# A Hymba layer on one core: the far blocks of attention exponentials are transposed by VectorE and a trip through memory

## The chip, the cores and the metric

The kernel runs on one core of a Trainium2 chip. The core has a TensorE (PE: matmuls; its weight loads are listed apart as PEld), a VectorE (DVE), a ScalarE (ACT), a GpSimd engine (POOL) and a SyncE (SP), which in this kernel issues most DMAs. Each engine works through its own instructions in order; between engines semaphores decide. The metric is the device time of one launch in microseconds (us); lower is better. Three runs of the kernel before gave 1260.56, 1261.29 and 1263.95 us, median 1261.29.

## The reference, cut to what matters

One layer over 1024 positions of width 1024. The change touches only the attention; the DeltaNet branch `B`, the convolutions and the norms are left out here.

```python
u = rms_norm(h, mix_norm_gain)
proj = u @ w_in                     # queries, keys, values of 8 heads of 64; q, k, v, gate of 4 DeltaNet heads
...
# A: each chunk of 64 positions sees itself and the 8 chunks before it
scores = einsum('bcqhd,bckhd->bchqk', qc, kb) * 64 ** -0.5 + bias[rel_idx]
scores = where(valid, scores, finfo.min)
p = softmax(scores, axis=-1)
o = einsum('bchqk,bckhd->bcqhd', p, vb)
o_att = rms_norm(o)
...
h = h + concat([o_att, o_dn], axis=-1) @ w_out
h = h + square(relu(rms_norm(h) @ w_ff1)) @ w_ff2
```

## The kernel before

The kernel runs in stages: the projections; then attention and DeltaNet together, mixed with the first parts of the output projection; then the output projection's rest and the two feed-forward products. The change lies in the second stage, about 350 to 575 us of the span.

**Tiling of the attention.** The 8 heads form two groups `g` of four, and the 1024 queries eight tiles `t` of 128 rows. A tile sees at most five blocks of 128 keys: the last two are *near* (`kb` to `t`), the `na = kb - k0` before them are *far*: none for tiles 0 and 1, one for tile 2, two for tile 3, three for tiles 4 to 7. Work goes in units `(g, t, pp)`, where `pp` is a pair of heads and `e` one head of it; `i = 2 * pp + e` counts the four heads of a group. Names in rows follow this: `t04_sa2` is group 0, tile 4, far scores of head 2.

**The steps of a unit.** `score` (line 931) computes scores on PE into PSUM banks (`sb` near, `sa` far; L927); DVE adds the bias, negates and takes the row minimum (L947 near into `pb`, L958 far into `pa`, the minimum goes to `nm`); ACT takes exponentials in place (L966 near, L970 far) and sums them. Queries lie on the partitions then, and the product with the values needs keys there. So `flip` (line 975) transposes: PE turns each 128x128 block against an identity into a PSUM bank of the pool `ps_t` (L987 near, L1003 far), and ACT or DVE, whichever the planner expects free sooner, copies the bank to memory on the chip (L993 to `tb`, L1008 to `ta`). `multiply` (line 1014, L1026) takes value blocks as weights and `ta`, `tb` as the moving operand, over all pairs and heads of a tile, into `t_o`. `finish` (line 1032) copies `t_o`, turns it back and divides by the sum.

**What sets the order.** The loop at line 1099 writes the program in the order of a planner: it keeps an expected time per engine (`pe`, `on`), per PSUM pool (`give`) and per unit (`ready`, `done`), and issues next what it expects to be ready first, with a rank for ties. Between units it puts DeltaNet steps and, late, output projections as fill. Two look-ahead limits hold `score` back: fewer than 5 units begun and not multiplied, fewer than 3 begun and not flipped. Pages of the pool `u` (24 of them) hold `pa`, `ta` and `pb`. In the list `turned` the far copies are noted; the output projection's fill uses it to be placed after them. Loads are issued by SP in program order, with the queries (L907), keys (L860), values and the DeltaNet operands (L629 to L635, L667, L702, L705) among them; eight completion semaphores (`DMAHW0` to `DMAHW7` in the rows) are taken in turn, and each DMA waits for the one that had its semaphore before.

## Time and profile before

| | |
|---|---|
| median of the runs | 1261.29 us |
| span of the profiled execution | 1256.3 us |
| first far scores of the stage | 371.1 us |
| first multiply with far keys (t02) | 386.24 us |
| multiply of the last tile of group 0 (t07) | 454.09 us |
| last multiply of the stage | 560.12 us |
| far transposes on PE, L1003 | 120, one 128x128 block each |
| far copies, L1008 | 48: 32 on ACT, 16 on DVE |

The profile is of one execution, and its span, from the first instruction to the last, is 5.0 us shorter than the median of the runs. Times in its rows are from the span's start. A matmul's record includes its drain, and records of matmuls overlap, so the sum of records is more than the time that PE spent; the distance between starts is what a matmul takes of PE. A group's row shows busy time, mean of one in ns, then the idle time of its engine ahead of it and what ended that. SP has no busy time in the profile; what its queue spends on issuing a DMA is shown in rows marked SPq.

### The profile page before, as it was taken

To read this page: it belongs to the slowest core of one execution; us is meant where nothing else is said; L and a number is where in the kernel's file an instruction comes from. 1 tells how busy PE (TensorE), PEld (TensorE's weight loads), DVE (VectorE), ACT (ScalarE), POOL (GpSimd) and SP (SyncE) were. 2 spreads that over 40 slices of the span, in tenths; PEclk is the share of its full clock that TensorE was granted. 3 is DMA by queue.
4 is the path that set the end of the run, shared out by engine and by line. 5 is a ranking of instruction groups with operands and counts; after the bars stand their busy time and mean duration, and the time that the engine had idled before them with its cause. 6 is when DMAs were issued, how large, how long until landed. Compare 5 with 4: busy or idle time off the path is not lost.

```text
span 1256.3 us, 17942 instructions
## 1 busy us (share of the span) xinstructions
PE 1236.3 (98%) x6686; PEld 1032.1 (82%) x6686; DVE 932.9 (74%) x1417; ACT 548.1 (44%) x899; POOL 270.5 (22%) x458
## 2 busy tenths in 40 slices
PE   9999999999999999899999999999999999999997
PEld 8778888788889988778888788888887888888886
DVE  7899987755237568776269766767769997997988
ACT  7233132232246756655365444454444543333330
POOL 4425552253133444523200000000000000000043
PEclk9999999999999999999999999999999999999999
DMA  7214364665585633045243333333269614333002
GB/s 228 63 41 141 101 164 118 119 161 134 168 259 136 189 85 88 24 135 176 76 143 104 114 118 118 119 132 101 84 205 365 202 67 134 105 97 101 1 34 100
DMA packets 134374, 158.52 MB, mean 126 GB/s; under 512 B 31120, under 2 KB 78224, under 8 KB 133776
## 3 DMA queue, kind: packets, MB, share of 16 engines
q1 hardware_dynamic: 116192, 135.11, 35.6%
q10 hardware_dynamic: 18096, 22.29, 5.2%
q8 instruction: 52, 0.85, 0.3%
q14 instruction: 34, 0.28, 0.1%
HBM read 109.91 MB, written 47.45 MB: 125 GB/s over the span
## 4 chain that ended last, share of the span: by engine, by line
PE 55%; DVE 5%; ACT 1%; issue 1%; POOL 0%; DVEq 0%; ACTq 0%
PE p L1444 24%; PE q L1348 21%; PE op L222 7%; PE t_o L1026 1%; DVE h L1290 1%; PE t_sa L927 0%; DVE q_0a_l L204 0%; PE t_tpb L987 0%; PE t_tpa L1003 0%; PE t_sb L927 0%; PE c_pv L516 0%; ACT t_pb L966 0%; PE c_po L516 0%; PE t_tpo L520 0%; PE c_pq L516 0%
## 5 line engine op out<-in xcount | busy, mean ns | idle before, releaser
L1516 POOL TENSOR_TENSOR y<-y,y 128x1024 f32<-128x1024 f32 x4 | 11.5, 2890 | 575.7 <-DVE y L1512 570.6
L1512 DVE TENSOR_TENSOR y<-y,p 128x1024 f32<-128x1024 f32 x46 | 55.1, 1217 | 5.4 <-PE p L1444 4.5
L222 PE MATMUL op<-ml,wo_h 128*128 128x512 f32 x128 | 50.2, 395 | 0.0
L222 PE MATMUL op<-mh,wo_h 128*128 128x512 f32 x128 | 49.2, 394 | 0.8 <-ACT mh L203 0.8
L222 PE MATMUL op<-mh,wo_l 128*128 128x512 f32 x128 | 49.3, 391 | 0.0
L947 DVE CUSTOM_DVE_ANT_0 t_pb<-t_sb,biasn 128x256 f32<-128x256 f32 (+1 forms) x64 | 23.2, 401 | 31.4 <-PE t_sb L927 31.3
L966 ACT ACTIVATE t_pb<-t_pb,t_nm 128x256 f32<-128x256 f32 (+1 forms) x64 | 31.4, 491 | 17.2 <-DVE t_nm L958 15.5
L1229 DVE TENSOR_TENSOR h<-op,op_x 128x512 f32<-128x512 f32 x16 | 10.8, 686 | 29.2 <-PE op L222 29.2
L1236 POOL TENSOR_TENSOR op_q<-op_q 128x512 f32<-128x512 f32 x14 | 19.6, 1400 | 55.4 <-ACT op_q L1235 55.1
L222 PEld LDWEIGHTS op<-mh,wo_h 128*128 128x128 f32 x128 | 23.9, 188 | 6.4 <-ACT mh L203 1.2
L222 PEld LDWEIGHTS op<-ml,wo_h 128*128 128x128 f32 x128 | 24.1, 188 | 5.0 <-DVE ml L204 0.2
L222 PEld LDWEIGHTS op<-mh,wo_l 128*128 128x128 f32 x128 | 24.1, 188 | 5.0
L958 DVE CUSTOM_DVE_ANT_0 t_pa<-t_sa,biaso,t_nm 128x384 f32<-128x384 f32 (+2 forms) x48 | 24.9, 543 | 2.8 <-PE t_sa L927 1.6
L970 ACT ACTIVATE t_pa<-t_pa,t_nm 128x384 f32<-128x384 f32 (+2 forms) x48 | 26.5, 552 | 0.0
L222 PE MATMUL aq_ps<-waq_h,ul 128*128 128x512 f32 x64 | 25.5, 399 | 0.0
L222 PE MATMUL dq_ps<-uh,wdq_h 128*128 128x512 f32 x64 | 25.5, 399 | 0.0
L222 PE MATMUL dv_ps<-ul,wdv_h 128*128 128x512 f32 x64 | 25.5, 399 | 0.0
L222 PE MATMUL dq_ps<-ul,wdq_h 128*128 128x512 f32 x64 | 25.3, 396 | 0.0
L222 PE MATMUL g_ps<-ul,wg_h 128*128 128x512 f32 x64 | 25.2, 394 | 0.0
L927 PE MATMUL t_sb<-ks,t_q 128*128 128x256 f32 (+1 forms) x144 | 24.0, 294 | 1.3 <-DVE t_nm L947 1.3
L222 PE MATMUL g_ps<-uh,wg_h 128*128 128x512 f32 x64 | 25.2, 394 | 0.0
L222 PE MATMUL aq_ps<-waq_h,uh 128*128 128x512 f32 x64 | 25.2, 396 | 0.0
(1109 smaller groups left out, 4304.3 us busy)
## 6 DMA issues: line engine op xcount, KB each, us to landing
wa<-in_w_ff_dram SPq DMA_DIRECT2D x32, 512.0 KB, 4.0
a<-in_w_ff_dram SPq DMA_DIRECT2D x32, 512.0 KB, 3.8
b<-f_dr SPq DMA_DIRECT2D x32, 512.0 KB, 3.4
f_dr<-yy ACTq DMA_DIRECT2D x16, 512.0 KB
t_q<-q_dr SPq DMA_DIRECT2D x30, 256.0 KB, 3.6
f_dr<-zz ACTq DMA_DIRECT2D x13, 512.0 KB
ks<-k_dr SPq DMA_DIRECT2D x16, 256.0 KB, 7.8
wo_r<-in_w_out_dram SPq DMA_DIRECT2D x16, 256.0 KB, 5.2
```

Of the source, the lines that this page charges most:

```text
L222: nc.tensor.matmul(ps, a, b, start=(first and i == 0), stop=(last and i == n - 1))
L927: nc.tensor.matmul(o, q[m][:, i * P:(i + 1) * P], k[:, c], start=(m == 0), stop=(m == 1))
L947: nc.vector.tensor_tensor_reduce(sb[:, c], bk[:, c], new[g][pp][:, c], -1.0, 3.0e38, ALU.add, ALU.min, nm[:, 4 + i:5 + i])
L958: nc.vector.tensor_tensor_reduce(sa[e][:, 0:wa], bk[:, 0:wa], old[g][i][:, 384 - wa:384], -1.0, nm[:, 4 + i:5 + i], ALU.add, ALU.min, nm[: ...
L966: nc.scalar.activation(sb[:, c], sb[:, c], AF.Exp, bias=m, scale=-1.0, accum_out=T["sums"][:, 4 + i:5 + i])
L970: nc.scalar.activation(sa[e][:, 0:wa], sa[e][:, 0:wa], AF.Exp, bias=m, scale=-1.0, accum_out=T["sums"][:, i:i + 1])
L1026: return nc.tensor.matmul(po[64 * e:64 * e + 64, pp * P:(pp + 1) * P], vt[k0 + j][:, 64 * h:64 * h + 64], (ta[e] if j < na else tb)[:, c:c ...
L1236: nc.gpsimd.tensor_tensor(acc, acc, sq, ALU.add)
L1290: nc.vector.tensor_tensor(t, wide(R[a], i), wide(R[b], i), ALU.subtract)
L1348: nc.tensor.matmul(part(ps, q), l[:, s], r, start=(k + m == 0), stop=(k == 3 and m == 2))
L1444: nc.tensor.matmul(part(ps[q], 0) if by_rows else part(ps[q // 2], q % 2), l[:, s], part(r, k), start=(i + k + m == 0), stop=(i + k + m == 4))
L1512: nc.vector.tensor_tensor(y[i][m], y[i][m], ps[m], op)
```

## The change

Far blocks no longer go through PE. Right after `score`, the new `turn_far` lets DVE transpose each head's `pa` within 32x32 blocks into a new page `tt` (L988 STREAM_TRANSPOSE, 48 of them: 32 of 128x384, 8 of 128x256, 8 of 128x128), and SP writes it to a buffer in DRAM (L991, one DMA a head). A later step, `land`, which the planner plans 3000 ns after the transposes' expected end, reads it back into `pa` with four DMAs a head (L1001), each 32 partitions with four runs of 32, 64 or 96 floats: this exchanges the blocks, so that keys lie on the partitions. `flip` keeps only the near blocks and is planned no earlier than 2500 ns ahead of the expected landing (`land`'s time plus 3500); `multiply` reads the far operand with a stride, four runs of 32 columns. The look-ahead limits go from 5 to 6 and from 3 to 5, and `turned` lists the near copies in place of the far ones. What is computed is the same.

```diff
@@ -972,6 +972,37 @@
                     done[e] = on("s", 480 + wa * 0.83, done[e])
             T["s"][pp] = sa, sb
 
+        def turn_far(g, t, pp):
+
+            T = tiles[g, t]
+            n, na = T["n"], T["kb"] - T["k0"]
+            u = begun
+            if not na:
+                landed[u] = 0
+                return
+            sa, _ = T["s"][pp]
+            sent = []
+            for e in range(2):
+                i = 2 * pp + e
+                tt = page("u", f"{n}_tt{i}")
+                nc.vector.transpose(tt[:, 0:na * P].rearrange("p (b j i) -> p j b i", b=4, i=32),
+                                    sa[e][:, 0:na * P].rearrange("p (j b i) -> p j b i", b=4, i=32))
+                p_dr = dram.tile([P, 4, na * 32], F32, name=f"{n}_dr{i}")
+                nc.sync.dma_start(out=p_dr, in_=tt[:, 0:na * P].rearrange("p (b r) -> p b r", b=4))
+                sent.append(p_dr)
+            at_ = on("v", 2 * (100 + na * 140), T["done"][pp][1])
+            sends.append((at_ + 3000, land, (u, g, t, pp, sent)))
+
+        def land(u, g, t, pp, sent):
+            T = tiles[g, t]
+            sa, _ = T["s"][pp]
+            for e in range(2):
+                for b in range(4):
+                    nc.sync.dma_start(
+                        out=sa[e][32 * b:32 * b + 32, 0:sent[e].shape[2] * 4].rearrange("j (a r) -> j a r", a=4),
+                        in_=sent[e][:, b, :].rearrange("(a j) r -> j a r", a=4))
+            landed[u] = clock.now + 3500
+
         def flip(g, t, pp):
             T = tiles[g, t]
             n, k0, kb = (T[k] for k in ("n", "k0", "kb"))
@@ -990,26 +1021,14 @@
             t = pe(nb * 218)
             e = clock.sooner(dict(s=140 + nb * 220, v=160 + nb * 270), t)
             with tc.high_priority():
-                copy[e](*w3)
+                ins = copy[e](*w3).ins
+            turned["vs".index(e)].append(ins)
             t = give("t", on(e, 140 + nb * 220, t, ahead=True))
             ta = [None, None]
             if na:
-                for e in range(2):
-                    i = 2 * pp + e
-                    yield 0, "t"
-                    tp = bank(ps_t, f"{n}_tpa{i}")
-                    for j in range(na):
-                        js = slice(j * P, (j + 1) * P)
-                        nc.tensor.transpose(tp[:, js], sa[e][:, js], ident)
-                    ta[e] = page("u", f"{n}_ta{i}")
-                    td = pe(na * 109)
-                    c = clock.sooner(dict(s=155 + na * 107, v=155 + na * 132), td)
-                    with tc.high_priority():
-                        ins = copy[c](ta[e][:, 0:na * P], tp[:, 0:na * P]).ins
-                    turned["vs".index(c)].append(ins)
-                    t = max(t, give("t", on(c, 155 + na * 132, td, ahead=True)))
+                ta = [x[:, 0:na * P].rearrange("p (a j i) -> p a j i", a=4, i=32) for x in sa]
             T["p"][pp] = ta, tb
-            ready.append(t)
+            ready.append(max(t, landed[len(ready)]))
 
         def multiply(g, t):
 
@@ -1022,9 +1041,10 @@
             def step(pp, j, e):
                 ta, tb = T["p"][pp]
                 h = 4 * g + 2 * pp + e
-                c = j * P if j < na else e * 256 + 256 - (na + nb - j) * P
+                c = e * 256 + 256 - (na + nb - j) * P
                 return nc.tensor.matmul(po[64 * e:64 * e + 64, pp * P:(pp + 1) * P],
-                                        vt[k0 + j][:, 64 * h:64 * h + 64], (ta[e] if j < na else tb)[:, c:c + P],
+                                        vt[k0 + j][:, 64 * h:64 * h + 64],
+                                        ta[e][:, :, j, :] if j < na else tb[:, c:c + P],
                                         start=(j == 0), stop=(j == na + nb - 1))
 
             held([(pp, j, e) for pp in (1, 0) for j in range(na + nb) for e in (1, 0)], step)
@@ -1074,7 +1094,7 @@
         units = [(g, t, pp) for g in range(2) for t in range(NT) for pp in range(2)]
         size = [min(t + 1, 5) for g, t, pp in units]
         total, spent, deltas, begun, multiplied = sum(size), 0, 0, 0, 0
-        ready, later, live = [], [], {}
+        ready, later, live, sends, landed = [], [], {}, [], {}
         banks = clock.banks
         start(0, 0)
         start(0, 1)
@@ -1113,12 +1133,14 @@
                     todo.append((max(t, banks["o"][0]), 1, "multiply"))
             for p in later[:1]:
                 todo.append((max(p[0], banks["t"][0]), 2, "later"))
-            if flipping is None and flipped < begun and flipped - multiplied < 2:
+            for p in sends[:1]:
+                todo.append((p[0], 2.5, "land"))
+            if flipping is None and flipped in landed and flipped - multiplied < 2:
                 flipping = flip(*units[flipped])
                 flipping = flipping, next(flipping)
             if flipping is not None:
-                todo.append((at(flipping[1]), 3, "flip"))
-            if begun < len(units) and begun - multiplied < 5 and (begun - flipped < 3):
+                todo.append((max(at(flipping[1]), landed[flipped] - 2500), 3, "flip"))
+            if begun < len(units) and begun - multiplied < 6 and (begun - flipped < 5):
                 a = banks["a"]
                 todo.append((max(a[0], a[1] - 500, a[2] - 900, tiles[units[begun][0:2]]["at"]), 4, "score"))
             if values_left:
@@ -1161,6 +1183,9 @@
                         later.sort(key=lambda p: p[0])
                 else:
                     give("t", on("v", 682, pe(440), ahead=True))
+            elif k == "land":
+                _, step, args = sends.pop(0)
+                step(*args)
             elif k == "flip":
                 want = next(flipping[0], None)
                 flipping = want and (flipping[0], want)
@@ -1169,6 +1194,7 @@
             elif k == "score":
                 g, t, pp = units[begun]
                 score(g, t, pp)
+                turn_far(g, t, pp)
                 begun += 1
                 if begun == len(units):
                     with tc.high_priority():
```

**On PE**, where tile 2 of group 0 is multiplied. Before, with the far operand from copies (`ta`) and steps of a DeltaNet chunk (`c0`, `c1`) between:

```order
L516 MATMUL c0_po_4159<-c0_vn_3901,c0_att_4113 128x128 [waits Activation_49]
...
L1026 MATMUL t02_o_4068<-t02_ta3_4034,vt0_3543 64x128 [waits DVE_49]
...
L1026 MATMUL t02_o_4068<-t02_ta2_3998,vt0_3543 64x128 [waits Activation_49]
L1026 MATMUL t02_o_4068<-t02_tb1_3994,vt1_3546 64x128 x2
L1026 MATMUL t02_o_4068<-t02_tb1_3994,vt2_3714 64x128 x2
L1026 MATMUL t02_o_4068<-t02_ta1_3920,vt0_3543 64x128
L1026 MATMUL t02_o_4068<-t02_ta0_3916,vt0_3543 64x128
...
L516 MATMUL c1_pS_4181<-c1_vn_4138,c1_kt_3981 128x128 [waits DVE_49]
...
L927 MATMUL t04_sb1_4226<-ks002_3531,t04_q_3826 128x128 [waits DVE_49,PE_49]
...
L927 MATMUL t04_sa2_4238<-ks002_3531,t04_q_3826 128x384 [waits DVE_49]
...
L927 MATMUL t04_sa3_4243<-ks003_3533,t04_q_3826 128x384 [waits DVE_49]
```

After, with the far operand from the DMAs (`pa`):

```order
L927 MATMUL t04_sa2_4137<-ks002_3531,t04_q_3842 128x384 [waits DVE_49]
...
L1045 MATMUL t02_o_4181<-t02_pa3_3828,vt0_3543 64x128 [waits DMAHW3_49,DMAHW4_49,DMAHW2_49,DMAHW1_49]
L1045 MATMUL t02_o_4181<-t02_pa2_3823,vt0_3543 64x128 [waits DMAHW0_49]
L1045 MATMUL t02_o_4181<-t02_tb1_4106,vt1_3546 64x128 x2
L1045 MATMUL t02_o_4181<-t02_tb1_4106,vt2_3714 64x128 x2
L1045 MATMUL t02_o_4181<-t02_pa1_3771,vt0_3543 64x128
L1045 MATMUL t02_o_4181<-t02_pa0_3766,vt0_3543 64x128 [waits DMAHW5_49]
...
L927 MATMUL t04_sa3_4142<-ks003_3533,t04_q_3842 128x384 [waits DVE_49]
...
L927 MATMUL t05_sb0_4309<-ks010_3847,t05_q_3961 128x256 [waits DMAHW5_49,DMAHW7_49,DVE_49,PE_49]
```

The multiply waits for DMAs now instead of DVE and ACT. It stood ahead of the scores of tile 4's second pair, and stands now between the far scores of that pair's two heads (`t04_sa2`, `t04_sa3`); the DeltaNet steps stand elsewhere.

**On DVE**, the scores of tile 5 of group 0 (each ISA row of L947 or L958 is followed by a small one that reads the minimum, left out). Before:

```order
L958 ISA t05_pa0_4316,t05_nm_3948<-t05_sa0_4313,biaso00_3698,t05_nm_3948 128x384 [waits DVE_49,PE_49]
...
L958 ISA t05_pa1_4321,t05_nm_3948<-t05_sa1_4318,biaso01_3702,t05_nm_3948 128x384 [waits DVE_49,PE_49]
...
L747 SCALAR_TENSOR_TENSOR state1_305<-state0_304,edec_807,c2_pS_4523 128x128 [waits PE_49]
...
L1053 TENSOR_TENSOR t00_on_3749<-t03_on_4301,t03_tot_4297 128x256 [waits PE_49]
L947 ISA t05_pb1_4371,t05_nm_3948<-t05_sb1_4370,biasn01_3539 128x256 [waits PE_49]
...
L958 ISA t05_pa2_4381,t05_nm_3948<-t05_sa2_4378,biaso02_3706,t05_nm_3948 128x384 [waits DVE_49,PE_49]
...
L958 ISA t05_pa3_4386,t05_nm_3948<-t05_sa3_4383,biaso03_3710,t05_nm_3948 128x384 [waits DVE_49,PE_49]
```

After:

```order
L958 ISA t05_pa0_4320,t05_nm_3965<-t05_sa0_4317,biaso00_3698,t05_nm_3965 128x384 [waits DMAHW1_49,DVE_49,PE_49]
...
L958 ISA t05_pa1_4325,t05_nm_3965<-t05_sa1_4322,biaso01_3702,t05_nm_3965 128x384 [waits DMAHW3_49,DVE_49,PE_49]
...
L1057 TENSOR_TENSOR t03_tot_4387<-t03_sum_3696 128x4
L1057 TENSOR_TENSOR t04_tot_4535<-t04_sum_3845 128x4
...
L988 STREAM_TRANSPOSE t05_tt0_4331<-t05_pa0_4320 128x3x4x32 [waits Activation_49]
L988 STREAM_TRANSPOSE t05_tt1_4335<-t05_pa1_4325 128x3x4x32 [waits Activation_49]
L947 ISA t05_pb1_4434,t05_nm_3965<-t05_sb1_4433,biasn01_3539 128x256 [waits PE_49]
...
L958 ISA t05_pa2_4444,t05_nm_3965<-t05_sa2_4441,biaso02_3706,t05_nm_3965 128x384 [waits DMAHW2_49,DVE_49,PE_49]
...
L958 ISA t05_pa3_4449,t05_nm_3965<-t05_sa3_4446,biaso03_3710,t05_nm_3965 128x384 [waits DMAHW4_49,DVE_49,PE_49]
...
L988 STREAM_TRANSPOSE t05_tt2_4455<-t05_pa2_4444 128x3x4x32 [waits DMAHW1_49,DMAHW6_49,DMAHW0_49,DMAHW7_49,PE_49,Activation_49]
L988 STREAM_TRANSPOSE t05_tt3_4459<-t05_pa3_4449 128x3x4x32 [waits DMAHW3_49,DMAHW5_49,PE_49,Activation_49]
```

Each pair of far score operations is now followed by two transposes that wait for ACT; the near scores of the next pair (`t05_pb1`) stand behind them. The third transpose also waits for DMAs and PE, since its page `tt` was another tile's.

**On SP**, around the loads of queries for tiles 4 to 6. Before:

```order
L907 DMA t04_q_3826<-q_dr_306 64x2x512 [waits DMAHW5_49,PE_49]
L907 DMA t04_q_3826<-q_dr_306 64x2x512 [waits DMAHW6_49]
L210 DMA wo0_6_r_6384<-in_w_out_dram 128x512 [waits DMAHW7_49,PE_49,Activation_49]
L667 DMA m4_sa_4591<-a_dr_312 64x4x64 [waits DMAHW0_49,PE_49]
L702 DMA c2_jq_4190<-dq_dr_309 128x512 [waits DMAHW1_49,PE_49]
L907 DMA t05_q_3944<-q_dr_306 64x2x512 [waits DMAHW2_49,PE_49]
```

After, the reads of tile 3 (`t03_pa`) and the writes of tile 4 (`t04_dr`):

```order
L907 DMA t06_q_4159<-q_dr_306 64x2x512 [waits DMAHW7_49]
L1001 DMA t03_pa2_3942<-t03_dr2_3955 32x4x64 [waits DMAHW0_49,Activation_49]
L1001 DMA t03_pa2_3942<-t03_dr2_3955 32x4x64 [waits DMAHW1_49]
L991 DMA t04_dr2_4153<-t04_tt2_4151 128x384 [waits DMAHW2_49,DVE_49]
L1001 DMA t03_pa2_3942<-t03_dr2_3955 32x4x64 [waits DMAHW3_49]
L991 DMA t04_dr3_4157<-t04_tt3_4155 128x384 [waits DMAHW4_49,DVE_49]
L1001 DMA t03_pa2_3942<-t03_dr2_3955 32x4x64 [waits DMAHW5_49]
L1001 DMA t03_pa3_3947<-t03_dr3_3959 32x4x64 [waits DMAHW6_49,Activation_49]
L1001 DMA t03_pa3_3947<-t03_dr3_3959 32x4x64 [waits DMAHW7_49]
```

The writes of heads 2 and 3 of tile 4, which wait for DVE's transposes, now stand between reads that bring tile 3's blocks back.

## The prediction

> **What bounds the kernel now.** I read the busy table at the head of the profile first, then the chain that ended last.
>
> ```profile
> span 1256.3 us, 17942 instructions
> PE 1236.3 (98%) x6686; PEld 1032.1 (82%) x6686; DVE 932.9 (74%) x1417; ACT 548.1 (44%) x899; POOL 270.5 (22%) x458
> PE 55%; DVE 5%; ACT 1%; issue 1%; POOL 0%; DVEq 0%; ACTq 0%
> ```
>
> TensorE (PE) is the bound: 98% busy, and more than half of the chain. The others have slack only on average, so I cut out the stage that the change touches. The next rows are the windows view: stretch, length, then busy time and instructions of PE, PEld, DVE, ACT and POOL, then granted TensorE clock, DMA share and GB/s. I cut at 454, where the last query tile of head group 0 (t07) starts its multiply, and end at 561, where the last multiply of the stage ends. The two rows behind them are the DMA part for the same stretches: packets, MB, share of the 16 engines.
>
> ```profile
> 371.00:454.00 83.00, 82.65 (x874) 75.88 (x873) 56.57 (x198) 54.80 (x164) 36.18 (x93) 1.00 0.58 158
> 454.00:561.00 107.00, 100.30 (x891) 88.12 (x890) 79.27 (x222) 68.18 (x194) 47.87 (x126) 1.00 0.27 79
> q1 hardware_dynamic: 11519, 12.92, 57.2%
> q1 hardware_dynamic: 5010, 8.26, 26.0%
> ```
>
> PE never rests in the first half (82.65 of 83) and rests 6.7 us in the second; the clock is at full speed in both. So work taken off PE is worth its full time, as long as its replacement is there when PE asks for it. The rest of the prediction is about that condition. DVE is at 68% and 74%. SP, whose queue issues the loads, appears in none of these columns: that is the resource to look up by itself.
>
> **The change, part by part.**
>
> (a) *Off PE: 120 transposes.*
>
> ```profile
> L1003 PE MATMUL t_tpa<-ident,t_pa 128*128 128x128 f32 x120 | 21.0, 278 | 1.4 <-ACT t_tb L993 1.4
> 495.54 0.49 PE L1003 MATMUL t_tpa<-ident,t_pa 128*128 128x128 f32 x3
> 495.87 0.60 PE L987 MATMUL t_tpb<-ident,t_pb 128*128 128x128 f32 x4
> ```
>
> 278 ns is one record with its drain, and matmuls overlap. The pitch counts: three transposes start at 495.54 and the next kind at 495.87, so 0.11 us each (0.109 over all of them). 120 x 0.109 = **13.1 us**, 6.5 us in each half. The wait of 1.4 us for a PSUM bank goes too; since near transposes still use those banks, I count it within the rounding (0 to -1.4).
>
> The Trainium skill, page "VectorE: DVE Perf Modes", section "Rules for kernel authors", speaks against the change: it wants a 128x128 transpose on TensorE where a PSUM destination will do. Its section "The three transpose paths" gives 390 ns on TensorE for a bf16 tile against 311 ns on VectorE, which does 32x32 blocks only. By its figures 120 tiles would be an estimated 46.8 us off PE and 37.3 us onto DVE; the trace's pitch of 0.109 us is less than a third of the first, and measurement decides.
>
> (b) *DVE: 48 block transposes more, 16 + 3 copies fewer.* No DVE transpose is in the trace. The nearest rows are DVE copies of the same shapes:
>
> ```profile
> L1008 DVE COPY t_ta<-t_tpa 128x384 f32<-128x384 f32 x11 | 6.0, 552 | 5.6 <-PE t_tpa L1003 5.6
> L1008 DVE COPY t_ta<-t_tpa 128x256 f32<-128x256 f32 x1 | 0.4, 424 | 0.0
> L1008 DVE COPY t_ta<-t_tpa 128x128 f32<-128x128 f32 x4 | 1.1, 284 | 0.2 <-PE t_tpa L1003 0.2
> L993 DVE COPY t_tb<-t_tpb 128x512 f32<-128x512 f32 x6 | 4.1, 686 | 4.1 <-PE t_o L1026 2.1 <-PE t_tpb L987 2.0
> L1395 DVE TENSOR_TENSOR wa<-wa,wa 128x1024 f32<-128x1024 f32 x8 | 9.8, 1224 | 0.2
> L384 DVE SCALAR_TENSOR_TENSOR dq_y<-dq_raw,cw,dq_y 128x512 f32<-128x512 f32 x24 | 20.5, 856 | 0.4
> ```
>
> 32 x 0.552 + 8 x 0.424 + 8 x 0.284 = 23.3 us, taking the copy's price. For the ends I count elements, 32 x 384 + 8 x 256 + 8 x 128 = 15,360 in a partition: the cheapest row by the element (1224 ns for 1024, 1.2 ns each) gives 18 us, the dearest (856 ns for 512, 1.67 ns each) 26 us. Off go 6.0 + 0.4 + 1.1 = 7.5 us of far copies and, by the new order, three near copies (3 x 0.686 = 2.1 us). Net +13.7 us busy, half in each half: first half 56.6 + 6.9 = 63.5 of 83, which fits.
>
> DVE takes its instructions in order, however, and each transpose waits for the exponentials of its head, which ACT works off in this time (one unit of two heads, first and last row):
>
> ```profile
> 502.56 0.51 ACT L966 ACTIVATE t_pb<-t_pb,t_nm 128x256 f32<-128x256 f32 x1 [0.37 <-DVE t_nm L958]
> ...
> 504.67 0.19 ACT L970 ACTIVATION_READ_ACCUMULATOR t_pa<-t_pa,t_nm 128x1 f32 x1
> ```
>
> That is 2.30 us from the first to the end of the last. DVE's second far score op of the unit (609 ns) covers 0.6, the first transpose 0.55, so DVE stands still for up to 1.15 us per unit where nothing lies between. In the new order one or two small rows lie between, so I take two thirds, 0.75: 24 units x 0.75 = 18 us, 9 in the first half. 63.5 + 9 = 72.5 of 83: DVE still fits, but the near and far score ops of the next unit stand behind the transpose, and PE needs their banks back. I charge 1.2 us for that in the first half (0 to 9).
>
> (c) *SP: 48 writes and 192 reads more.* This is the term that decides. What SP's queue takes per issue:
>
> ```profile
> L577 SPq DMA_DIRECT2D a_dr<-d_A x8: 327/332/333, 94.8 to 190.4; - x8
> DMA to landing us min/median/max: 2.0/2.0/2.1
> L635 SPq DMA_DIRECT2D l_w<-y_dr x16: 302/388/476, 246.2 to 377.2; - x16
> DMA to landing us min/median/max: 2.0/4.7/7.3
> L667 SPq DMA_DIRECT2D m_sa<-a_dr x8: 584/594/1089, 252.9 to 430.0; - x8
> DMA to landing us min/median/max: 3.6/4.0/6.2
> 377.65 1.16 SPq L907 DMA_DIRECT2D t_q<-q_dr  x2
> 378.92 0.52 SPq L210 DMA_DIRECT2D wo_r<-in_w_out_dram  x1
> ...
> 385.54 0.80 SPq L630 DMA_DIRECT2D l_xa<-a_dr  x1
> 454.09 0.88 PE L1026 MATMUL t_o<-t_ta,vt 128*64 128x128 f32 x12
> ```
>
> A write is a plain store like L577: 0.33 us. A read is 32 partitions with four short runs each; L635 (32 partitions, short runs) is the nearest: **0.39 us**, with 0.30 (its fastest) and 0.59 (L667, also short runs) as ends. Over the stage 48 x 0.33 + 192 x 0.39 = 91 us of SP time that was not there.
>
> In the first half, from the place where the first read stands in the new order to the last read for t07: 24 writes x 0.33 = 7.9, 96 reads x 0.39 = 37.4, and 47 issues that were there already. The eleven from 378.92 to the end of 385.54's take 5.7 us, 0.52 each, so 47 x 0.52 = 24.4. Sum 69.7. SP is busy with older work until 377.65, so without any wait the last read is issued at 447.4. But the queue is in order too: the new order puts the write of t04's fourth head among t03's reads; it waits for a score that PE holds behind t02's multiply, and that for t02's reads. The same loop stands at t05 and t06. I charge 8 us for these waits (0 to 16, at some 2.7 each: one ACT unit of 2.30 and a piece of DVE). Then 455.4, plus a landing of 3.5 us (2.0 to 7.3 by the rows), plus the 1.2 us of (b): t07's multiply starts at **460.1 instead of 454.09, +6.0**. If SP kept up, it would start 6.5 us earlier; so PE is to rest some 12.5 us there.
>
> The DMA engines behind SP fill up as well: the 24 heads of the half are 16 of 384 columns, 4 of 256 and 4 of 128, 3.93 MB written and as much read. 7.9 MB on 12.92 MB at 57.2% would be 92% at the same price for a byte. I don't add a term for it, since it shows first in the landings, but I take their upper end of 7.3 us for the range.
>
> (d) *Second half.* PE saves 6.5 us again. DMA share is 26.0%, SP's old load is thinner, and each unit's chain from last score to multiply is: ACT 2.3 and transposes 1.1 and a wait on either, together 4.5; a write 0.33 and its landing 2.0; eight reads 3.1; landing 3.0: 12.9 us. What PE has to do between a tile's last score and its multiply is 10 to 13 us there (the rows that the new order puts between, at the trace's pitches), middle 11.5, so it waits 1.4 us for each of the six tiles with far keys that multiply there: 8.4 - 6.5 = **+1.9** (-6.5 if all of it is covered). Behind the stage nothing changes in kind. The near copies that move to ACT are hidden: ACT is at 68 of 107.
>
> (e) *Multiply.* The far operand is now read as four runs of 32 columns instead of one of 128. No row shows this; far and near multiplies read contiguous runs at equal price, so I take nothing, with a doubling as the other end (rival 4).
>
> Sum: +6.0 + 1.9 = +7.9 on the span: 1264.2. The median of the runs, 1261.29, lies 5.0 above the profiled span, and I add this: **1269 us**.
>
> **Rivals.** 0.3% (3.8 us) is about what a measurement of this kernel can tell from no change.
>
> 1. *SP keeps up* (the other side). If a read takes 0.30 and the writes' waits vanish, the first half's SP work is 7.9 + 28.8 + 24.4 = 61.1, the last read goes at 438.8 and lands before 447.6, which is when PE would want it (454.09 - 6.5). Then nothing replaces the 13.1 us; I leave 3 us for DVE: 1261.3 - 10 = 1251. It decides at the point where SP's sum of work and waits falls under 66 us. For it: the forecast misses that point by 12 us only, out of estimates. Against: two in-order queues and PE wait for each other in a ring.
> 2. *Costs cancel*: between the two, 1257.5 to 1265. For it: the same sum with 2 us of waits behind SP's writes instead of 8.
> 3. *Reads at L667's price*: 96 x 0.20 = 19 us more in the first half, 1269 + 19 = 1288. For it: 594 is what several short runs with 64 partitions took; against: 32 partitions took 388.
> 4. *The strided operand eats the gain*, so that the change takes nothing off PE.
>
> ```profile
> L1026 PE MATMUL t_o<-t_ta,vt 128*64 128x128 f32 x240 | 19.1, 278 | 0.1
> 454.79 0.61 PE L1026 MATMUL t_o<-t_tb,vt 128*64 128x128 f32 x8
> ```
>
> Twelve far records start within 454.79 - 454.09 = 0.70 us, 0.058 each; doubled, 240 x 0.058 = 14 us. Half of it is hidden where PE waits for reads anyway: 1269 + 7 = 1276.
>
> 5. *The clock falls.* If PE rests several us at a time, the granted clock may go down and what follows is slower. The longest rest in the stage is this, at a clock of 1.00:
>
> ```profile
> 509.97 1.16 PE L516 MATMUL c_pk<-state,kT 128*128 128x128 f32 x8 [1.44 <-DVE c_jv L711]
> ```
>
> Nothing here shows a longer rest or a lower clock. My 12.5 us of PE rest in the first half come in pieces of about 3 us; if each of four were followed by a rest's length at half speed, it would cost 4 x 1.5 = 6 us: 1275. The Trainium skill, page "TensorE: Matmul & The Clock Gate", Part 1, has such a rule: after an idle window of about 3.4 us the clock goes to half until it has been busy as long; by it pieces under that length cost nothing, and the trace agrees as far as its 1.44 us go.
>
> **How the numbers follow.** Slower, as forecast, 0.38; rival 3, 0.10; rival 4, 0.03; rival 5, 0.04: slower 0.55. Rival 2 (within 0.3%) 0.18; rival 1, 0.27. The range: of rival 1 I leave out what lies under 1249 (0.09: 13.1 us of PE and more), above I reach over rival 3 to 1294, with landings at their 7.3 as well (0.09 left out). The slower cases by themselves span 1265 to 1294.
>
> **What would show it.** (a) no far transposes among PE's groups, and PE's busy time down by about 20 us of records; (b) the transposes near 0.55 us for 384 columns, and DVE idle before them put down to ACT's exponentials; (c) SP's reads at 0.39 us, back to back until about 455, and PE's idle time before the far multiplies put down to DMA, together over 10 us in the first half; t07's multiply near 460; (d) a second half of about 109 us. I am wrong if PE does not wait at the far multiplies of t04 to t07 (rival 1), if far multiplies start at over 0.09 us pitch (rival 4), or if the windows show a clock under 1.00 (rival 5).

## The result, and the profile after

The changed kernel takes 1294.41 us (median of four runs, 1292.74 to 1297.8) against 1261.05 for the kernel before: slower by a ratio of 1.0266, 95% interval 1.0246 to 1.0287, or 33 us. Forecast were 1269 and a range up to 1294. The direction was right, the size was not: a slowdown of 8 us was forecast, and 33 were measured.

The head of the page of the changed kernel, span and busy time by engine:

```profile
span 1295.8 us, 18110 instructions
PE 1240.9 (96%) x6566; PEld 1033.7 (80%) x6566; DVE 946.6 (73%) x1446; ACT 539.2 (42%) x870; POOL 274.0 (21%) x458
```

The spans differ by 39.5 us, 6 more than the medians. A run's time is some 2 us above its span, and the execution profiled here took 1297.8 us, the slowest of the four. The 5.0 us that the prediction added is more than these 2, since it also holds that the profiled execution of the kernel before was faster than the median.

Two numbers of the page carry the account. PE's **rests**, span less busy, went from 1256.3 - 1236.3 = 20.0 to 1295.8 - 1240.9 = 54.9 us, 34.9 more. PE's **busy time** should have fallen by the 13.1 us of 120 transposes and rose by 4.6: 17.7 us of stretching of the work that stayed. 34.9 + 17.7 - 13.1 = 39.5. This sum closes by the way in which the stretch is reckoned, so it proves nothing by itself. What tests it is the clock: in the stretches of the span in which the granted clock was 0.50 PE was busy for 37.4 us, and at half speed half of that, 18.7 us, is loss. That is within 1 us of the 17.7.

The same two stretches as before, cut at the multiplies of the new trace (columns as there: stretch, length, PE, PEld, DVE, ACT, POOL, granted clock, DMA share, GB/s):

```profile
371.00:480.80 109.80, 85.34 (x794) 76.93 (x793) 63.19 (x222) 52.02 (x163) 29.23 (x74) 0.83 0.68 183
480.80:590.00 109.20, 94.43 (x826) 84.48 (x827) 81.13 (x221) 59.19 (x163) 56.08 (x142) 0.95 0.56 153
```

The first half grew from 83 to 110 us, PE rests 24 us in it, and the clock is 0.83 where it was 1.00. Next, the first row of the waits view for PE in the stage (in total, times, longest):

```profile
PE t_o L1045 <- DMA t_pa<-t_dr: 26.4, 8, 7.3
```

and the multiplies of tiles 5 and 7 on PE's timeline:

```profile
449.34 1.61 PE L1045 MATMUL t_o<-t_pa,vt 128*64 128x128 f32 x12 [7.27 <-DMA t_pa<-t_dr]
480.80 0.88 PE L1045 MATMUL t_o<-t_pa,vt 128*64 128x128 f32 x12
```

PE stands 7.27 us for one tile's blocks, and then its twelve matmuls take 1.61 us where tile 7's take 0.88, as before: they run at half the clock (0.50 in these windows, shown further down). The rows for the two lines of SP's queue (duration of an issue, least, median and most, then first and last start), the second with the time from issue to landing:

```profile
L991 SPq DMA_DIRECT2D t_dr<-t_tt x48: 319/376/1732, 378.6 to 574.2; - x48
L1001 SPq DMA_DIRECT2D t_pa<-t_dr x192: 302/430/2979, 381.4 to 583.8; - x192
DMA to landing us min/median/max: 1.7/2.4/5.0
```

and a piece of SP's timeline ahead of tile 5's multiply:

```profile
439.39 0.52 SPq L907 DMA_DIRECT2D t_q<-q_dr  x1
439.96 5.74 SPq L1001 DMA_DIRECT2D t_pa<-t_dr  x6
446.54 0.34 SPq L991 DMA_DIRECT2D t_dr<-t_tt  x1
446.95 0.89 SPq L1001 DMA_DIRECT2D t_pa<-t_dr  x2
```

SP issues one behind the other; the write at 446.54, which had to wait for its transpose, stands between the sixth and the seventh read of the pair that PE wants. That transpose had itself waited 2.47 us for a page whose earlier write had not landed. A row's time here runs from the first issue to the end of the last: of the 5.74 us only 2.57 are the six issues, and most of the rest are waits for earlier loads (queries and keys) that still hold the completion semaphores. Last, the first matmuls of the output projection and of the first feed-forward product, by their tiles, in the kernel before:

```profile
L222 PE MATMUL op<-mh,wo_h x128: 387/390/504, 537.8 to 632.0; 128*128 128x512 f32 x128
L1348 PE MATMUL q<-b11h,q_0a_h x8: 388/389/392, 632.7 to 637.5; 128*128 128x512 f32 x8
```

and in the changed kernel:

```profile
L222 PE MATMUL op<-mh,wo_h x128: 387/390/501, 573.8 to 668.9; 128*128 128x512 f32 x128
L1374 PE MATMUL q<-b11h,q_0a_h x8: 389/389/392, 669.6 to 674.3; 128*128 128x512 f32 x8
```

t07's multiply is 26.7 us late (480.80 against 454.09), the last multiply of the stage 29.6 (589.10 against 559.47 for the last far one), the feed-forward 36.9: the stage got less of the output projection into it (47 of its matmuls and 11.5 us of PE, where before it were 73 and 18.2), and that came behind.

### The profile page after: what moved, and what is told of

Its sections match the earlier page's. It is cut to its first block, busy times and chain, and to the rows that moved or that the text cites. A ratio compares the mean times of both kernels' runs of the same rounds, so it can differ in the third digit from the quotient of the medians.

```text
span 1295.8 us, 18110 instructions
## 1 busy us (share of the span) xinstructions
PE 1240.9 (96%) x6566; PEld 1033.7 (80%) x6566; DVE 946.6 (73%) x1446; ACT 539.2 (42%) x870; POOL 274.0 (21%) x458
## 4 chain that ended last, share of the span: by engine, by line
PE 50%; DVE 3%; DMA 1%; issue 1%; POOL 0%; ACT 0%; SPq 0%; POOLq 0%; DVEq 0%
PE p L1470 23%; PE q L1374 22%; PE op L222 5%; DMA wa<-in_w_ff_dram 1%; DVE ml L204 1%; DMA wo_r<-in_w_out_dram 0%; DVE b22l L204 0%; DVE q_0a_l L204 0%; DVE t2l L204 0%; DVE a L1562 0%; DVE z L1394 0%; DVE b L1549 0%; DVE h L1255 0%; PE hrow L1338 0%; DVE h L1316 0%
## 5 line engine op out<-in xcount | busy, mean ns | idle before, releaser
L1542 POOL TENSOR_TENSOR y<-y,y 128x1024 f32<-128x1024 f32 x4 | 11.5, 2892 | 578.3 <-DVE y L1538 573.2
L1045 PE MATMUL t_o<-t_pa,vt 128*64 128x128 f32 x240 | 25.2, 338 | 27.5 <-DMA t_pa<-t_dr 26.4
L947 DVE CUSTOM_DVE_ANT_0 t_pb<-t_sb,biasn 128x256 f32<-128x256 f32 (+1 forms) x64 | 23.0, 395 | 34.5 <-PE t_sb L927 30.5
L1045 PEld LDWEIGHTS t_o<-t_pa,vt 128*64 128x64 f32 x240 | 20.0, 175 | 30.2 <-DMA t_pa<-t_dr 22.7
L966 ACT ACTIVATE t_pb<-t_pb,t_nm 128x256 f32<-128x256 f32 (+1 forms) x64 | 31.3, 489 | 28.5 <-DVE t_nm L958 24.6
L988 DVE STREAM_TRANSPOSE t_tt<-t_pa 128x384 f32<-128x384 f32 (+2 forms) x48 | 23.7, 502 | 13.7 <-ACT t_pa L970 9.2
L1262 POOL TENSOR_TENSOR op_q<-op_q 128x512 f32<-128x512 f32 x14 | 20.1, 1438 | 59.0 <-ACT op_q L1261 58.9
L958 DVE CUSTOM_DVE_ANT_0 t_pa<-t_sa,biaso,t_nm 128x384 f32<-128x384 f32 (+2 forms) x48 | 24.7, 545 | 10.5 <-PE t_sa L927 6.2
L927 PE MATMUL t_sa<-ks,t_q 128*128 128x256 f32 (+2 forms) x128 | 23.8, 311 | 2.1 <-DVE t_nm L958 2.0
```

The costliest lines, as they stand in the source:

```text
L927: nc.tensor.matmul(o, q[m][:, i * P:(i + 1) * P], k[:, c], start=(m == 0), stop=(m == 1))
L947: nc.vector.tensor_tensor_reduce(sb[:, c], bk[:, c], new[g][pp][:, c], -1.0, 3.0e38, ALU.add, ALU.min, nm[:, 4 + i:5 + i])
L958: nc.vector.tensor_tensor_reduce(sa[e][:, 0:wa], bk[:, 0:wa], old[g][i][:, 384 - wa:384], -1.0, nm[:, 4 + i:5 + i], ALU.add, ALU.min, nm[: ...
L966: nc.scalar.activation(sb[:, c], sb[:, c], AF.Exp, bias=m, scale=-1.0, accum_out=T["sums"][:, 4 + i:5 + i])
L988: nc.vector.transpose(tt[:, 0:na * P].rearrange("p (b j i) -> p j b i", b=4, i=32), sa[e][:, 0:na * P].rearrange("p (j b i) -> p j b i", b ...
L1045: return nc.tensor.matmul(po[64 * e:64 * e + 64, pp * P:(pp + 1) * P], vt[k0 + j][:, 64 * h:64 * h + 64], ta[e][:, :, j, :] if j < na else ...
```

## The experiments

The expectations name theories by letters. A: the number of issues on SP's queue makes the blocks late. B: their short runs do, on the DMA engines. C: DVE does, standing at its transposes. D and E: PE's rests at the far multiplies are the loss itself, with the clock that falls in them (D), or only where a ring of waits through PE, DVE, ACT and the trip becomes visible (E); in the expectation of no_wait the letter E stands for what is D here. F: the trip's load makes other loads late. G: the order in SP's queue does it, reads behind writes that wait.

All kernels in one table. "Rest" is span less PE's busy time, "stretch" is PE's busy time above its work at full clock (1223.2 us without the 120 transposes, 1236.3 with them), both from the page of one execution. In most rows the stretch is the clock's: half of PE's busy time at clock 0.50 comes within 2.1 us of it. Two rows are otherwise, far_last (12.5 us by the clock) and no_wait (15.3): some 8 and 5 us of their stretch lie at full clock, and what they are is not shown.

| kernel | median us | before, same chip | ratio, 95% interval | rest | stretch |
|---|---|---|---|---|---|
| before | 1261.05 | | | 20.0 | 0 |
| changed | 1294.41 | 1261.05 | 1.0246 to 1.0287 | 54.9 | 17.7 |
| no_turn | 1300.65 | 1261.59 | 1.0299 to 1.0337 | 56.0 | 16.4 |
| no_trip | 1258.27 | 1261.59 | 0.9968 to 0.9996 | 29.9 | 3.6 |
| bare | 1256.56 | 1263.51 | 0.9921 to 0.9962 | 26.7 | 5.1 |
| long_runs | 1294.09 | 1261.73 | 1.0235 to 1.0291 | 50.4 | 14.3 |
| one_read | 1284.48 | 1261.59 | 1.0170 to 1.0211 | 48.2 | 12.0 |
| one_read_short_runs | 1271.35 | 1261.59 | 1.0067 to 1.0103 | 36.1 | 11.1 |
| reads_act | 1299.05 | 1261.73 | 1.0257 to 1.0318 | 51.2 | 17.3 |
| writes_pool | 1290.10 | 1260.33 | 1.0212 to 1.0265 | 49.0 | 14.2 |
| one_read_w_pool | 1269.72 | 1260.33 | 1.0049 to 1.0089 | 36.1 | 9.1 |
| spread | 1288.96 | 1260.33 | 1.0196 to 1.0257 | 44.2 | 17.1 |
| far_last | 1292.75 | 1261.73 | 1.0219 to 1.0261 | 44.9 | 20.2 |
| no_wait | 1292.61 | 1263.51 | 1.0212 to 1.0246 | 47.9 | 20.1 |
| ahead_5_3 | 1304.26 | 1261.73 | 1.0296 to 1.0367 | 59.0 | 15.1 |
| before_3_2 | 1270.77 | 1263.51 | 1.0045 to 1.0077 | 28.5 | 3.0 |

One caution for reading it: the program's order is made anew for each kernel, so that an edit also moves other rows. By the traces 45 of PE's 6566 matmuls stand in another place in long_runs than in the changed kernel, and some 900 to 2400 in the others. one_read and one_read_short_runs, which theory A wanted within 4 us of each other, differ by 13 us; a difference of that size between kernels of different orders is not the edit's for certain.

### Is it DVE, and what is the most that the change could bring?

no_turn: DVE transposes nothing.

```diff
-                tt = page("u", f"{n}_tt{i}")
-                nc.vector.transpose(tt[:, 0:na * P]..., sa[e][:, 0:na * P]...)
-                nc.sync.dma_start(out=p_dr, in_=tt[:, 0:na * P]...)
+                nc.sync.dma_start(out=p_dr, in_=sa[e][:, 0:na * P]...)
```

> The changed kernel without DVE's block transposes: the exponentials go to memory as they are and come back with blocks exchanged but not transposed within. All 240 DMAs stay, DVE has 24 us less and no wait for ACT. Theories A and B: within 8 us of the changed kernel, 1286 to 1296 (the writes can go a little earlier). Theory C: falls below 1270.

Measured 1300.65: no gain, rather 6 us worse. DVE's transposes, its standing for ACT and the extra pages are not the loss; theory C wanted a time below 1270.

no_trip: DVE transposes, no DMA. bare: the same, and no transposes by anyone (lines 986 to 992 go as a whole).

```diff
-                p_dr = dram.tile([P, 4, na * 32], F32, name=f"{n}_dr{i}")
-                nc.sync.dma_start(out=p_dr, in_=tt[:, 0:na * P]...)
...
-                    nc.sync.dma_start(out=sa[e][32 * b:32 * b + 32, ...], in_=sent[e][:, b, :]...)
```

> The changed kernel without its DMAs: DVE transposes into the extra page, nothing is written or read back, and the multiply uses the exponentials untransposed. The order of the program stays. PE saves its 13.1 us, and DVE has its 24 us and its waits for ACT. Theories A and B: nothing to wait for at the multiplies, 1248 to 1256. Theory C: stays above 1275, since DVE stands as before.

> The kernel without a trip, and without the block transposes on DVE as well: far blocks are not transposed by anyone, which leaves that out of the computation; planner, limits and the rest of the changed kernel stay. It shows what taking 120 transposes off PE can bring at most in this plan. If PE's work is what counts: 13.1 us under before, 1246 to 1250. If PE rests elsewhere as soon as it has less to do (in the kernel without a trip it rested 9 us more than before and lost 4 by the clock): 1254 to 1260.

Measured 1258.27 and 1256.56. The head of no_trip's page:

```profile
span 1256.7 us, 17698 instructions
PE 1226.8 (98%) x6566; PEld 1020.5 (81%) x6566; DVE 945.6 (75%) x1446; ACT 537.6 (43%) x870; POOL 272.3 (22%) x458
```

and of bare's:

```profile
span 1255.0 us, 17648 instructions
PE 1228.3 (98%) x6566; PEld 1022.8 (82%) x6566; DVE 926.2 (74%) x1398; ACT 537.6 (43%) x870; POOL 271.7 (22%) x458
```

So the trip is the loss: 36 us between no_trip and the changed kernel. And without it the gain is not 13.1 us, only 3 to 7: in the profiles PE rests 6.7 to 9.9 us more than before and is stretched by 3.6 to 5.1. no_trip misses the 1248 to 1256 of theories A and B by 2 us; bare came out where PE was expected to rest elsewhere. In no_trip the longest of it by the waits view is this, for a norm's result on DVE:

```profile
PE t_tpo L520 <- DVE t_on L1072: 9.3, 3, 5.9
```

### Short runs, or the number of issues?

long_runs: the same four reads a head, in whole rows.

```diff
-                        in_=sent[e][:, b, :].rearrange("(a j) r -> j a r", a=4))
+                        in_=sent[e][32 * b:32 * b + 32])
```

> The changed kernel with each of its four reads a head taking 32 whole rows of the buffer, 1536 bytes a run, in place of four runs of 384; the exchange of blocks is left out, so the attention comes from blocks that are transposed within only. 192 reads, same bytes, a quarter of the runs; the order on PE differs in nine short moves. Theory A (SP's queue, by the number of issues): 1286 to 1296, as the changed kernel. Theory B (short runs on the DMA engines make landings late): 1265 to 1282.

one_read, one contiguous read a head; one_read_short_runs, one read in 512 short runs.

```diff
-                for b in range(4):
-                    nc.sync.dma_start(out=sa[e][32 * b:32 * b + 32, ...], in_=sent[e][:, b, :]...)
+                nc.sync.dma_start(out=sa[e][:, ...].rearrange("p (a r) -> p a r", a=4), in_=sent[e])
```

> Each head's block comes back with one read of 128 contiguous partitions in place of four reads of 32 partitions in short runs; blocks are not exchanged, so the attention is computed from blocks that are transposed within but not between each other. Same bytes, same program order otherwise: 48 reads instead of 192, 128 runs a head instead of 512. Theory A (SP's queue: the 96 reads of the first half took 53 us of SP, 0.56 each, and PE's rests and the half clock follow from it): some 40 us of SP work go in the first half, PE finds its blocks there, time 1248 to 1262. Theory B (the DMA engines: short runs make landings late): falls as well, 1250 to 1270. Theory C (DVE stands at the transposes for ACT and for pages, and scores and writes are late by it): stays at 1280 to 1294.

```diff
+                r = sent[e].shape[2] - 2
+                nc.sync.dma_start(out=sa[e][:, ...].rearrange("p (a r) -> p a r", a=4)[:, :, 0:r], in_=sent[e][:, :, 0:r])
```

> As the kernel with one read a head, but each read leaves out the last two columns of every 32-column group of its head's page, so that it moves 512 short runs again, with 48 issues on SP. Two columns in each run and the exchange of blocks are left out of the computation. Theory A: within 4 us of the kernel with one contiguous read. Theory B: near the changed kernel, 1284 to 1294. Theory C: 1280 to 1294, like the one with a contiguous read.

long_runs, which nearly keeps the order, stays at 1294.09: short runs (theory B) cost nothing that can be measured. One read in place of four brings 10 and 23 us, not the 32 to 46 that theory A forecast for one_read, and the kernel with short runs came out the faster one. one_read's 1284.48 lies in the range of theory C, which no_turn rules out; 1271.35 lies in nobody's range. That both are faster by more than the spread of their runs speaks for the number of issues as a part of the loss, not as all of it; the order may have a share in both. The bytes of the trip are the same in one_read and, but for a sixteenth, in one_read_short_runs, so what the bytes cost the DMA engines (share 0.68 in the changed kernel's first half, 0.58 before) can't be the main part.

### Whose queue, and in what order?

reads_act puts the 192 reads on ACT's queue, writes_pool the 48 writes on POOL's, one_read_w_pool does the latter to one_read, and spread puts the writes on POOL's and half of the reads on ACT's.

```diff
-                nc.sync.dma_start(out=p_dr, in_=tt[:, 0:na * P]...)
+                nc.gpsimd.dma_start(out=p_dr, in_=tt[:, 0:na * P]...)
...
-                    nc.sync.dma_start(
+                    (nc.sync, nc.scalar)[e].dma_start(
```

> The changed kernel with its 192 reads issued from ACT's queue instead of SP's. SP loses 53 us of work in the first half, ACT gains as much and is in order as well, so its exponentials stand behind reads that wait for writes. Theory A (SP's queue is what makes the blocks late): 1265 to 1285. Theory E (the ring through ACT, DVE, the write, the read and PE is what it costs, wherever the reads are issued): 1290 to 1320.

> The changed kernel with its 48 writes issued from POOL's queue instead of SP's. No read stands behind a write that waits for a transpose any more; SP keeps 192 reads. Theory G (SP's queue order: reads stand behind writes that wait): 1270 to 1285. Theory A (the sum of SP's issues): SP loses 10 of some 90 us of work in the first half, 1284 to 1292. If POOL's issues cost it much, or its own work stands behind the writes: 1295 to 1310.

> The kernel with one contiguous read a head, which leaves out the exchange of blocks, with its writes issued from POOL's queue. SP is left with 48 issues more than before. Theory G: the blocks arrive in time, 1255 to 1268. If the length of the trip itself (two landings) is what PE waits for: 1276 to 1290, as with the writes on SP.

> The changed kernel with its writes on POOL's queue, the reads of each pair's first head on SP's and of the second on ACT's; the result is the same. SP has 96 more issues than before instead of 240. Theory A: 1268 to 1282. If ACT's exponentials behind its reads make up for it, as with all reads on ACT: 1290 to 1305.

Reads on ACT: 1299.05, nothing gained, where theory A forecast 1265 to 1285; ACT is in order too, and now its exponentials stand behind reads (in its trace one of L966 waits 4.54 us for `t_pa<-t_dr`). Writes on POOL: 4 us, and not the 9 to 24 of theory G. Writes on POOL and half of the reads on ACT: 5 us, where theory A forecast 1268 to 1282. Only with 48 reads do writes on POOL matter: 1269.72 against 1284.48, which lies between the two ranges of its expectation. That would fit theory G (reads behind writes that wait), but 15 us is also the size of what the order alone can do, and one_read_short_runs came to 1271.35 with its writes on SP, so I don't call it shown. What is shown: 48 reads and no write on SP come to within 10 us of before; 192 reads come to no better than 1289, whichever of the queues tried here has them. And PE's waits for reads don't decide: by the waits views they are 26.4 us in the changed kernel, 11.1 in reads_act, 8.9 in writes_pool and 7.1 in spread, at nearly the same time.

### Does PE's wait for its own blocks make the loss?

far_last multiplies pair 0 before pair 1 and near before far blocks; no_wait lets the reads land in a page that nobody uses; ahead_5_3 takes the look-ahead limits back.

```diff
-            held([(pp, j, e) for pp in (1, 0) for j in range(na + nb) for e in (1, 0)], step)
+            held([(pp, j, e) for pp in (0, 1) for j in js for e in (1, 0)], step)
```

```diff
-                        out=sa[e][32 * b:32 * b + 32, 0:sent[e].shape[2] * 4].rearrange("j (a r) -> j a r", a=4),
+                        out=tt[32 * b:32 * b + 32, 0:p_dr.shape[2] * 4].rearrange("j (a r) -> j a r", a=4),
```

> The changed kernel, with the multiply of a tile in another order: pair 0 before pair 1 and near blocks before far ones, so that PE has 1.6 us of work at each tile (20 matmuls of pair 0 and 8 near ones of pair 1 at 0.058) before it needs the block that lands last. The same result is computed. Theory D (PE's rests at the far multiplies and the clock that falls in them are the loss, whatever makes the blocks late): the eight rests of 26.4 us shrink by up to 1.6 each, 10 to 13 us, and some of the half clock goes: 1270 to 1284. Theory E (a ring: what PE does earlier makes nothing land earlier, it only waits at the next tile instead): 1288 to 1296.

> The changed kernel with all of its transposes, writes and reads, but the reads land in the page that the block was written from, which nobody uses again, and the multiply takes the exponentials untransposed. SP and the DMA engines have the same load, PE waits for no read. Theory E (the loss is PE's wait for its own blocks, and the clock that falls in it): 1255 to 1266, within 6 us of the kernel without a trip. Theory F (the load on SP makes other loads late, queries and DeltaNet operands, and these cost): 1275 to 1292.

```diff
-            if begun < len(units) and begun - multiplied < 6 and (begun - flipped < 5):
+            if begun < len(units) and begun - multiplied < 5 and (begun - flipped < 3):
```

> The changed kernel with the look-ahead limits of before, 5 units begun and not multiplied and 3 begun and not flipped. Less other work lies between a unit's scores and its multiply. Theories A and E both: PE rests longer, 1300 to 1330; if the limits are no part of it, 1290 to 1298.

far_last: 1292.75, in the range of theory E and not in D's. PE waits 18.1 us for reads there, 8 less than in the changed kernel, and the median moves by 2. no_wait was the surprise: 1292.61, as slow as the changed kernel, without a single wait of PE for a read (DVE waits 6.6 us for pages that the reads still hold; the 3.3 us in the second row below follow from that). Its waits on PE, the longest first:

```profile
PE c_tpo L520 <- DVE c_o L795: 13.1, 1, 13.1
PE t_sa L927 <- DVE t_nm L958: 3.7, 2, 3.3
PE t_sb L927 <- DMA t_q<-q_dr: 2.8, 2, 2.3
```

and a piece of its timeline for SP:

```profile
560.04 5.63 SPq L1002 DMA_DIRECT2D t_tt<-t_dr  x6
565.77 0.38 SPq L702 DMA_DIRECT2D c_jg<-dg_dr  x1
566.19 6.16 SPq L210 DMA_DIRECT2D wo_r<-in_w_out_dram  x5
```

The loads of the output projection's weights stand behind six reads, of which the third waits 2.9 us for a write to land. ACT then stands 9.4 us for the first of these loads, DVE stands for ACT, and the result that PE waits 13.1 us for stands behind that on DVE. PE waits for queries elsewhere. So theory D (E in this expectation) falls: taking PE's wait for its blocks away gains nothing here, and other loads are late in its place (theory F, whose range ended at 1292). That the queue holds back whatever comes next is what this one trace shows; that it would be so in any order is not shown. ahead_5_3 is 10 us worse, as forecast for a trip that needs the raised limits, though a difference of that size can be the order's too.

### Is the clock an effect of the rests?

before_3_2 is the kernel before with shorter look-ahead: the same work, more rests.

```diff
-            if begun < len(units) and begun - multiplied < 5 and (begun - flipped < 3):
+            if begun < len(units) and begun - multiplied < 3 and (begun - flipped < 2):
```

> The kernel before with look-ahead limits of 3 and 2 in place of 5 and 3: same work, no transposes on DVE, no trip, but PE finds less to do between a unit's scores and its multiply and rests more. It tests the account of the clock apart from the change: the span should grow by the rests that are added plus half of the time in which PE works at clock 0.50, to within 2 us, and the clock should be 0.50 only behind stretches of 3.4 us in which PE was busy less than about half. If the clock is no part of it, the span grows by the rests alone. By size: 1270 to 1300.

Its page:

```profile
span 1267.8 us, 17946 instructions
PE 1239.3 (98%) x6686; PEld 1033.2 (81%) x6686; DVE 933.4 (74%) x1419; ACT 547.6 (43%) x897; POOL 269.4 (21%) x458
```

8.5 us more rests and 3.0 us more busy time for the same matmuls, together its 11.5 us of span. The expectation wanted the rests plus half of PE's busy time at 0.50, to within 2 us: that half is 3.9 us and the sum 12.4. Each time the clock fell behind a window that was busy for less than half. So the clock's part follows rests without the change and with the same matmuls; 1270.77 is the low end of what was forecast. The windows view of the changed kernel, cut every 3.41 us around the long wait (columns as above; the last three are clock, DMA share and GB/s; 441.31 to 448.13 is left out):

```profile
431.07:434.48 3.41, 3.40 (x52) 2.96 (x51) 3.19 (x10) 2.93 (x8) 1.46 (x8) 1.00 0.41 98
434.48:437.89 3.41, 1.41 (x14) 1.11 (x15) 1.73 (x5) 1.06 (x4) 2.66 (x9) 1.00 0.73 224
437.89:441.31 3.42, 2.75 (x17) 2.15 (x16) 0.63 (x2) 1.15 (x5) 0.00 (x0) 0.50 0.96 220
...
448.13:451.55 3.42, 2.21 (x21) 2.21 (x23) 1.50 (x7) 0.00 (x0) 0.00 (x0) 0.50 0.78 252
451.55:454.96 3.41, 3.41 (x28) 3.08 (x25) 2.05 (x8) 2.66 (x9) 0.00 (x0) 0.50 0.61 142
454.96:458.38 3.42, 3.42 (x32) 3.30 (x30) 2.99 (x10) 0.81 (x2) 0.00 (x0) 1.00 0.42 133
```

and two windows of the kernel before, on whose border its longest wait (1.88 us, up to 229.99) lies:

```profile
225.01:228.42 3.41, 3.10 (x14) 2.25 (x12) 3.27 (x14) 0.27 (x1) 1.75 (x1) 1.00 0.00 0
228.42:231.83 3.41, 1.84 (x10) 1.63 (x11) 3.31 (x16) 1.00 (x2) 1.64 (x1) 1.00 0.00 0
```

Behind a window with 1.41 us of PE work the clock is 0.50; it comes back behind a window that was full. The window of before with 1.84 us of work, 54% of it, cost nothing: the clock stayed at 1.00.

## Why the prediction was wrong

- **(a) Off PE, 13.1 us: right.** The transposes are gone. In bare, which lost little by the clock, PE's busy time fell by 8.0 us, and with the 5.9 that half its busy time at 0.50 makes, 13.9 us of work went. The sign that was named for the changed kernel, PE's busy time down by about 20 us, did not come: it rose by 4.6, by the clock. And a saving on the bound engine came through only in part even without the trip (bare, no_trip: 3 to 7 us by the medians).
- **(b) DVE: busy time right.** It rose by 13.7 us (946.6 - 932.9), as forecast. The block transposes:

```profile
L988 DVE STREAM_TRANSPOSE t_tt<-t_pa 128x384 f32<-128x384 f32 x32 | 18.0, 570 | 10.3 <-ACT t_pa L970 7.6 <-DMA t_dr<-t_tt 2.5
```

  570 ns against the 552 taken from the copy. DVE stood 9.2 us for ACT ahead of all 48, half of the 18 forecast, and another 9.4 us, which were not forecast, for pages whose writes had not landed. no_turn, without any of this, is no faster.
- **(c) SP: the right place, the sum too small.** This is the first step that failed. The last read for t07 was to be issued by 455.4 and t07's multiply to start at 460.1; they came at 479 and 480.80. Summed over SP's rows from 378.6 to the end of that read at 479.0: 96 reads 44.9 us (0.47 each, not 0.39), 24 writes 10.3 (0.43, not 0.33), 47 other issues 23.5 (24.4 forecast), 9.7 us in gaps of under 0.12 us between issues, which the sum by durations left out, and 12.1 us of longer waits (8 forecast). Together 100.4 us, where the prediction had 77.7; without the longer waits 88.3 where it had 69.7. About half of the longer waits SP's waits view puts down to earlier loads, for which the prediction had no term. Of the 26.7 us by which t07's multiply is late, PE's rests make 24.1 and the clock 12.1; 6.5 went off with the transposes and some 3 with work that now stands elsewhere. Only 17.5 of these rests are waits for reads (12.5 were forecast): the prediction also took the far multiply for the only one to suffer, and no_wait shows that other loads behind the reads are late as well.
- **Rival 5, the clock: the second, and as large.** It got a chance of 0.04, a price of 6 us and no place in the sum; it costs 17.7 us of the profiled 39.5. The rests in that rival were right in kind (the eight at the far multiplies are 1.3 to 7.3 us long). The step that failed is that the sum had no term for the clock, because pieces under some 3.4 us were taken to be free. This was drawn from the Trainium skill, page "TensorE: Matmul & The Clock Gate", Part 1, which has the clock go to half after an idle window of about 3.4 us; the traces show windows of that length, but a window that is less than about half busy is enough (56 of 56 below 45%, as counted at the end). The row of before with its wait of 1.44 us could not tell that.
- **(d) Second half: the length right by luck.** 109.2 us against a forecast of about 109. PE's waits for reads were right, 8.9 us against 8.4. But the clock cost some 4.9 us that were not forecast, and about as much was gone from the stage: it held 6.6 us less of the output projection, which began at 573.8 instead of 537.8, and 7.3 us (36.9 - 29.6) came behind it. "Behind the stage nothing changes in kind" was wrong.
- **(e) The strided operand costs nothing: right**, 0.88 us for twelve as before.

The sum with what was measured: -13.1 + 34.9 of rests + 17.7 of clock, where the prediction had -13.1, 21 of rests and none. Of the 34.9 the waits for reads at the far multiplies are 26.4; the other 8.5 lie elsewhere. Rival 3 (reads at 0.59, 1288) was the nearest of the cases in its number, not in its mechanism: reads took 0.47. What is not settled: how much of the rests is the number of SP's issues and how much their order. A version that beats the kernel before wasn't found, and bare, which transposes nothing, shows about 7 us to be had in this plan as it stands.

## What to carry to other kernels

Work that is taken off the bound engine and put into many small DMAs must be counted on the queue that issues them, with the gaps between issues and everything else that this queue has to bring; taking away one wait behind a full queue can just move it to the next load, as in no_wait. Read rests of the bound engine together with its clock: here 34.9 us of new rests came with 17.7 us of slower matmuls. Before such a trade, leave the work out altogether, as bare does: it shows in one run how little there is to gain.

## What the runs showed of the hardware that was not expected

TensorE's clock goes by fixed windows of 3.41 us: in each of the sixteen profiles, every change of the granted clock lies a whole number of 3.413 us behind the one before. What counts is how busy PE was in the window, not the length of one rest. Over all sixteen profiles, the last 10 us of each left out, of the windows at full clock in which PE was busy for less than 45% all 56 were followed by a window at 0.50; of those from 45 to 50% 14 of 21, from 50 to 55% 2 of 21, from 55 to 90% 16 of 256, and of 5422 busier ones none. From 0.50 the clock came back behind 74 of 82 windows that were at least 90% busy, and behind 14 of 65 that were less. What decides in the windows between is not shown.

So a rest of 3.0 us cost nothing in no_turn, where a border cut it into two windows that were 54 and 58% busy:

```profile
226.71:230.12 3.41, 1.86 (x9) 1.20 (x7) 3.27 (x13) 0.69 (x1) 1.75 (x1) 1.00 0.00 0
230.12:233.54 3.42, 1.98 (x11) 1.72 (x12) 3.32 (x16) 0.59 (x1) 1.64 (x1) 1.00 0.00 0
233.54:236.95 3.41, 3.41 (x17) 2.81 (x16) 3.27 (x11) 0.00 (x0) 1.70 (x1) 1.00 0.65 140
```

In one_read_short_runs two rests of 0.73 and 1.20 us fell into one window, which was 43% busy, and the next one had half the clock:

```profile
509.02:512.43 3.41, 1.48 (x12) 1.09 (x12) 3.41 (x12) 2.20 (x7) 1.23 (x7) 1.00 0.67 190
512.43:515.84 3.41, 3.41 (x34) 3.41 (x36) 2.78 (x10) 0.00 (x0) 3.00 (x11) 0.50 0.96 259
```

A window at 0.50 costs up to 1.7 us, half of its length, and up to five came in a row in the changed kernel (437.9 to 455.0 us).
